# When merged rows are squared, when weight scales may be taken, and how the last tile is cut, in a streaming-encoder block

## The chip, the cores and the metric

The kernel runs on one core of one Trainium2 chip. Its time is device microseconds of one execution, and the profile is one execution of it on the same kind of core. TensorE (PE) multiplies, VectorE (DVE) and ScalarE (ACT) and GpSimd (POOL) work elementwise, SyncE (SP), ACT and POOL also issue DMAs. Each engine takes its own instructions strictly in the order in which the program gives them.

## The reference, cut to what matters

```python
x = x + 0.5 * swiglu_ffn(rms_norm(x, g1), w1_in, w1_out)          # FFN 1, 1024 rows of 1024, width 2816
h = rms_norm(x, g_mix)
o_a = sparse_attention(h) @ w_o_a                                 # three mixers read h
glu_a, glu_b = split(gelu(s5(h)) @ w_glu)
o_b = glu_a * sigmoid(glu_b)
o_m = memory_attention(h) @ w_o_m
g = sigmoid(gates(h))                                             # three gates per channel
merged = g[0] * o_a + g[1] * o_b + g[2] * o_m                     # where the branches meet
x = x + merged @ w_out
x = x + 0.5 * swiglu_ffn(rms_norm(x, g2), w2_in, w2_out)          # FFN 2
return rms_norm(x, g_final)
```

## The kernel before

Activations lie transposed: 128 channels on the partitions, 1024 positions along the free axis, handled in two halves of 512. Every product is made from two half-precision parts of each operand (high and low), as three fp16 matmuls that add up in one PSUM bank (`matmul3`). A weight block is loaded, its squares are summed on ACT and DVE, a power-of-two scale is taken from the sum, and the block is split into the two parts (ACT writes the high part, DVE the low one). The sum crosses the partitions by a tiny matmul with a matrix of ones into a bank called `ms`; this matmul stands in PE's queue like all others. An activation tile that is to be multiplied later goes the same way: `Rows.steps` squares it on ACT, takes its scale on DVE, writes the high part on ACT and the low part on DVE, a stage at each call of `Rows.more()`.

**Who sets the order.** The order of all instructions is fixed when the program is written out, by a planner with a cost model of its own (`Model`, `Sched`). Main work runs as a generator that yields after each group of matmuls; at each yield `Stream.prep` gives out steps of the next weight blocks, if the modelled time has come (`WBlock.can`) and the engine is modelled to be less than `BACKLOG` us behind. `WBlock.LATE` is an extra modelled time that must go by between a block's squares and its scale, so its `ms` matmul; it is 0 until FFN 2's Strassen part, where it becomes 2.5. If a block is wanted before its steps are done, `go` gives out all that is left at once.

**Where the branches meet** (in `mixer`, `for n in range(2 * ND)`): 16 units, for 8 slices of 128 channels and 2 halves each. A unit has 30 matmuls of 512 columns: 6 into `gb` (bank `lg`), 6 into `ga` (bank `mm`, two buffers), 6 into `pm` (bank `ao`, one buffer), 12 into `po` (bank `mm`). ACT takes each bank to SBUF: `sb` (with Tanh), `gc`, `sm`, and the output tile `m`; `sb`, `sm` and `gc` come from one ring `t2` of four buffers. DVE combines `sb` with `gc`, with its gate, `sm` with its gate, and `m` with its gate (two SBUF inputs each); POOL adds `sb` and `sm`, and then that sum to `m`. The last part (`rest`) of a unit is given out in the next unit. After the second half, `rest` calls `Rows.put` at once: ACT's square of the merged slice, which reads POOL's sum, stands in ACT's queue there, ahead of the next unit's Tanh, `gc` and `sm`. The tiles of the loop lie in `xa`, cut in 16 places of 512: gates in 0 to 8, merged slices in 9 to 14.

**Out of the mixers** (`out_stage`): 16 tiles of 512 columns, first the four tiles of two slices with the first six of eight rows, later the last two rows (`begun`, `ended`); `norm_forms` then prepares FFN 2's input (half 0 first) on DVE, ACT and POOL while PE multiplies the rest.

**FFN 2's second chunk** takes 11 rows of hidden width per tile; the first weight block is cut in 9 and 2 rows (`out_block`). Finished tiles are turned back by PE transposes, multiplied by the last gain and scaled by their norm (`final`, `turn`), and each 128 positions are stored by one DMA of 512 KB from SP. `between`, called in the midst of the next tile's matmuls, does all of a finished tile's turn; the last tile's turn comes after all matmuls.

Of the kernel before, what the change touches and what calls it, by code (L numbers as in the profile page):

```python
# [21 lines left out]
HT = 512  # L22
# [537 lines left out]
class Rows:  # L560
# [6 lines left out]
        self.inv2 = kb.const.tile([P, nk], F32, name=tag + "j")  # L567
        self.n, self.at, self.late, self.apart = 0, {}, [], False

    def put(self, k, src, mul=None):  # L570

        self.late += [self.steps(k, src, mul)]
        self.more()

    def more(self):
# [4 lines left out]
        while self.late:  # L580
            self.more()

    def steps(self, k, src, mul):
        kb, nc = self.kb, self.kb.nc
        t = kb.small.tile([P, 3], F32, name="rsc", tag="rsc", bufs=4)
        hl = self.t[k] = self.room(k)
        nc.scalar.activation(kb.junk(S), src, AF.Square, accum_out=t[:, 0:1])
        yield None
        kb.pow2(t[:, 0:1], t[:, 1:2], t[:, 2:3])
        inv = self.inv[:, k:k + 1]  # L590
        if mul is None:
            nc.vector.tensor_scalar(inv, t[:, 1:2], INV_MUL, None, op0=OP.mult)
        else:
            nc.vector.tensor_scalar(inv, t[:, 1:2], INV_MUL, mul, op0=OP.mult, op1=OP.mult)
        nc.vector.tensor_tensor(self.inv2[:, k:k + 1], inv, inv, op=OP.mult)
        if self.apart:
            yield None
        nc.scalar.activation(hl[:, 0], src, AF.Copy, scale=t[:, 2:3])
        yield None
        nc.vector.scalar_tensor_tensor(hl[:, 1], src, t[:, 2:3], hl[:, 0], op0=OP.mult, op1=OP.subtract)  # L600
        self.n, self.at[k] = k + 1, nc.t["vector"] + 0.12
# [5 lines left out]
class Builder:  # L607
# [348 lines left out]

    def out_block(self, w, rows, uses, first=0, apart=False):

        n = rows.nk - 2
        return self.rows_block(w, rows, uses, ((first, n - first), (n, 2)), apart)  # L960

    def rows_block(self, w, rows, uses, cuts, apart=False):
        return WBlock(self, [Seg([(0, w[k0 * P:(k0 + nk) * P])], nk, w.shape[1], rows, mul=0.5, k0=k0)
# [205 lines left out]
    def out_stage(self, blocks, rows, new_xo, xd_in, per, m, done, first=1, cut=(0, HT), between=None):  # L1169
# [4 lines left out]
        xo = {}  # L1174
        order = [(d, half, slice(0, HT)) for d, half in self.tail_order(ND, m)]
        d, half, _ = order.pop()
# [9 lines left out]
        def begun(n, d, half, s):  # L1186
            w = blocks[d // per]
            c = (d % per) * P
            yield from self.stream.begin(w, 1)
            acc, x, t = self.mm()[:, s], rows.x(half), xo[d, half][:, s]  # L1190
            g = w.segs[0]
            cuts = [0, *range(2, g.nk, 2), g.nk]
            for k0, k1 in zip(cuts, cuts[1:]):
                self.matmul3(acc, lambda i, k: g.hl[:, i, k, c:c + P], lambda i, k: x(i, g.k0 + k)[:, s], g.nk, ks=range(k0, k1))
                rows.more()
                if k0 == (4 if s.stop - s.start == HT else cuts[-2]) and between is not None:
                    between()
                yield None
            if len(w.segs) == 1:
                accs[n] = acc  # L1200
                return
            nc.vector.scalar_tensor_tensor(t, acc, g.inv, t, op0=OP.mult, op1=OP.add)
# [1012 lines left out]
    def mixer(self, w, xa, ss, xd_in, xd_out, after):  # L2215
# [87 lines left out]
        heads = lambda t, half: lambda i, k: t[:, 4 * half:4 * half + 4, 2 * k + i]  # L2303
        gates, mt, xf = {}, {}, xa.rearrange("p k a h t -> p (k a h t)")
        room = lambda i, n: xf[:, i * HT:(i + n) * HT].rearrange("p (j t) -> p j t", j=n)

        def g_in(n):
            if n < 2 * ND:
# [6 lines left out]
        late = []  # L2315
        for n in range(2 * ND):
            d, half = divmod(n, 2)
            b = w["go"][d // 2]
            glu, wm, wa = b.segs
            c = (d % 2) * P  # L2320
            yield from self.stream.begin(b)
            gb, ga = self.bank("lg"), self.mm()
            self.matmul3(gb, lambda i, k: glu.hl[:, i, k, 256 + c:256 + c + P], w["y"].x(half), 2)
            if late:
                late.pop()()
            yield None
            self.matmul3(ga, lambda i, k: glu.hl[:, i, k, c:c + P], w["y"].x(half), 2)
            sb, sm, gc = self.t2("sb"), self.t2("sm"), self.t2("gc")
            nc.scalar.activation(sb, gb, AF.Tanh, scale=glu.inv)
            yield None  # L2330
            w["m"].more()
# [10 lines left out]
            nc.vector.scalar_tensor_tensor(sm, tm, 1.0, sm, op0=OP.add, op1=OP.mult)  # L2342
            nc.gpsimd.tensor_tensor(sb, sb, sm, op=OP.add)
            w["m"].more()
            yield None
            self.matmul3(po, lambda i, k: wa.hl[:, i, k, c:c + P], heads(qS, half), 4, ks=range(2, 4))
            self.stream.end(b)
# [3 lines left out]
            def rest(d=d, half=half, wa=wa, po=po, ta=ta, sb=sb):  # L2351
                m = mt[d][:, half]
                nc.scalar.activation(m, po, AF.Copy, scale=wa.inv)
                nc.vector.scalar_tensor_tensor(m, ta, 1.0, m, op0=OP.add, op1=OP.mult)
                nc.gpsimd.tensor_tensor(m, m, sb, op=OP.add)
                if half == 1:
                    w["m"].put(d, mt[d].rearrange("p h t -> p (h t)"))

            late.append(rest)
            yield None  # L2360
        w["out"][0].go(("split", 0))
        late.pop()()
        self.stream.BACKLOG = 3
        nc.free.add(xa.tensor.name)
        en.close()
        xo, F = after()
        pool = m3.enter_context(tc.tile_pool(name="xo4", bufs=1, side="right"))
        xo = xo + [pool.tile([P, HT], F32, name="xo4", tag=f"xo4{i}") for i in range(3)]
        xo = iter([xo[i % len(xo)] for i in range(2 * ND)])
# [5 lines left out]
    def final(self, xt, ss, gb, out):  # L2375

        nc = self.nc
        late, sums = [], {}

        def between():  # L2380
            if late:
                turn(*late.pop(0))

        def turn(d, half, c, xn):
            n = (c.stop - c.start) // P
# [11 lines left out]
            if d == ND - 2:  # L2397
                sums[half] = self.vss[:, 4 * half:4 * half + 4]
                nc.vector.tensor_scalar(sums[half], self.row_sums(ss[half]), 1.0 / D, EPS, op0=OP.mult, op1=OP.add)
            if d == ND - 1:  # L2400
                i0 = c.start // P
                nc.vector.scalar_tensor_tensor(v, v, 1.0 / D, sums[half][:, i0:i0 + n], op0=OP.mult, op1=OP.add)
                self.rsqrt(y, v, "n")
                for i in range(n):
                    t = t0 + i
                    if i < 3 * n // 4:
                        nc.vector.tensor_scalar(xt[:, t], xt[:, t], y[:, i:i + 1], None, op0=OP.mult)
                    else:
                        nc.scalar.activation(xt[:, t], xt[:, t], AF.Copy, scale=y[:, i:i + 1])
                    nc.sync.dma_start(out[t * P:(t + 1) * P], xt[:, t])  # L2410

        def done(d, half, c, acc, w, xo):
            xn = self.t2("xn")
            nc.vector.scalar_tensor_tensor(xn[:, c], acc, w.inv, xo, op0=OP.mult, op1=OP.add)
            if d < ND - 1:
                self.square_add(ss[half], sp(xn), d == 0)
            late.append((d, half, c, xn))
            yield None

        return done, between  # L2420


@with_exitstack
def tile_hybrid_block(ctx, tc, x, mem, ffn1_norm, ffn1_w_in, ffn1_w_out, mix_norm, w_in, a_q_gain, a_k_gain, rel_bias,
# [4 lines left out]
    kb = Builder(ctx, tc)  # L2429
# [61 lines left out]
    def main():  # L2491
# [6 lines left out]
        with ExitStack() as en:  # L2498
# [19 lines left out]
            def ring(kind):  # L2518
                n[kind] += 1
                i = n[kind] - 1  # L2520
                if kind == "xo":
                    return F["xo"][i % 4]
                if kind == "gt":
                    i = 8 + 2 * (i % 2)
                    return tiles[:, i:i + 2].rearrange("p i t -> p (i t)")
                return tiles[:, i % 8]
# [12 lines left out]
            nc.gpsimd.dma_start(gb, final_norm.to_broadcast([P, D]))  # L2539
            xt = F["all"].rearrange("p n k j t -> p (n k j t)").bitcast(F32)[:, 0:S * D // P].rearrange("p (i n) -> p i n", n=D)  # L2540
            done, between = kb.final(xt, ss, gb, out[0])
            yield from kb.out_stage(b2[-1], g2, lambda: ring("xo"), xd[2], 2, 2, done, 3, between=between)
            between()

    sched.add(setup(), 1)
# [32 lines left out]
```

## Time and profile before

| | us |
|---|---|
| median of three runs (lowest, highest) | 2257.52 (2257.22, 2260.11) |
| the profiled execution's own time | 2257.12 |
| its span, first to last instruction | 2255.0 |
| PE busy in the span | 2140.5 (95%) |
| DVE, ACT, POOL busy | 1347.8, 1186.8, 396.2 |

Times in the rows are microseconds from the span's start, and mean durations are nanoseconds. A row of the timeline has start, duration, engine, line, instruction, tile written and tiles read, shapes and count; square brackets tell how long the engine stood idle before it and whose work ended that. PE's granted clock is given as a share of 2.4 GHz, so 0.5 is 1.2 GHz.

### The profile page before, as it was taken

Reading aid. Unit: us, or ns where it says so; the run is one execution under the profiler, and the core shown is the slowest. Engines: PE = TensorE matmul, PEld = TensorE weight load, DVE = VectorE, ACT = ScalarE, POOL = GpSimd, SP = SyncE. Lnnn points to the kernel's source line nnn. Section 1 sums busy time; section 2 is a strip of 40 time slices with the busy share of each in tenths; the row PEclk is TensorE's granted clock in tenths of the full one; section 3 lists DMA queues with packets and bytes.
Section 4 is the critical chain, followed back from the end, with each engine's and each line's share of the span. In section 5 each row is a group of like instructions: output and inputs, shape, how many; then the busy total and the mean of one; then the engine's idle time right before and its main releaser. Section 6 shows DMA issues by size and latency. Waiting matters only on the chain. (4 is left out here: it accounts for less than half of the span.)

```text
span 2255.0 us, 33448 instructions
## 1 busy us (share of the span) xinstructions
PE 2140.5 (95%) x12585; PEld 1141.1 (51%) x12589; DVE 1347.8 (60%) x3669; ACT 1186.8 (53%) x2367; POOL 396.2 (18%) x582
## 2 busy tenths in 40 slices
PE   6999999999999889979999999898999999999997
PEld 3555444444444556656556674333854444444443
DVE  6446852344555467677669886675756643466653
ACT  6543434344444488778877766544555432455421
POOL 1200130000000103312200004410254301344100
PEclk9999999999999999999999999999999999999999
DMA  6422231202222102123321204334111234112222
GB/s 224 120 82 82 64 103 57 63 26 80 89 89 85 52 20 79 40 66 108 122 86 58 65 37 152 117 120 119 43 57 57 70 123 125 47 57 64 81 62 93
DMA packets 204066, 185.18 MB, mean 82 GB/s; under 512 B 7376, under 2 KB 176528, under 8 KB 203264
## 3 DMA queue, kind: packets, MB, share of 16 engines
q1 hardware_dynamic: 185904, 135.84, 19.1%
q0 software_dynamic: 8416, 29.36, 4.1%
q10 hardware_dynamic: 9584, 17.85, 2.7%
q8 instruction: 98, 1.61, 0.3%
q14 instruction: 64, 0.52, 0.1%
HBM read 143.57 MB, written 40.50 MB: 82 GB/s over the span
## 5 line engine op out<-in xcount | busy, mean ns | idle before, releaser
L62 PEld LDWEIGHTS <-wh 128*128 128x128 f16 x8412 | 817.3, 98 | 949.5 <-issue 38.0
L62 PE MATMUL mm<-xa,wh 128*128 128x512 f16 x2376 | 540.0, 380 | 6.5 <-ACT xa L62 4.9
L62 PE MATMUL lg<-xa,wh 128*128 128x512 f16 x1080 | 242.6, 379 | 0.4 <-DVE xn L62 0.4
L62 ACT ACTIVATE junk<-wf 128x1024 f16<-128x1024 f32 (+3 forms) x292 | 194.0, 664 | 35.7 <-DMA wf<-in_ffn_w_in_dram 20.1
L62 PE MATMUL mm<-G,wh 128*128 128x512 f16 x960 | 210.5, 379 | 0.0
L62 DVE SCALAR_TENSOR_TENSOR wh<-wf,wsc,wh 128x1024 f16<-128x1024 f32 (+1 forms) x132 | 176.3, 1337 | 49.3 <-ACT wh L62 49.1
L62 PE MATMUL mm<-H,wh 128*128 128x512 f16 x864 | 197.3, 383 | 6.8 <-ACT wh L62 5.2
L62 PE MATMUL lg<-F,wh 128*128 128x512 f16 (+1 forms) x900 | 179.4, 353 | 0.0
L62 ACT ACTIVATE wh<-wf,wrs 128x128 f16<-128x128 f32 (+2 forms) x304 | 112.4, 438 | 103.4 <-DVE wrs L62 94.0
L62 ACT ACTIVATE wh<-wf,wsc 128x1024 f16<-128x1024 f32 (+1 forms) x132 | 139.1, 1060 | 33.3 <-DVE wsc L62 23.3
L62 PE MATMUL mm<-wh,xa 128*128 128x256 f16 (+2 forms) x1152 | 129.1, 271 | 13.9 <-ACT us L62 7.8
L62 PE MATMUL mm<-F,wh 128*128 128x512 f16 (+1 forms) x672 | 129.2, 347 | 0.0
L62 PEld LDWEIGHTS <-xa 128*128 128x128 f16 x1152 | 108.2, 106 | 32.1 <-issue 15.4
L62 DVE SCALAR_TENSOR_TENSOR wh<-wf,wrs,wh 128x128 f16<-128x128 f32 (+2 forms) x304 | 112.9, 423 | 12.7 <-ACT wh L62 11.5
L62 DVE SCALAR_TENSOR_TENSOR gt<-lg,wsc,si 128x512 f32<-128x512 f32 x44 | 33.0, 749 | 129.6 <-PE lg L62 110.5
L62 PE MATMUL ao<-F,wh 128*128 128x512 f16 x456 | 104.6, 379 | 0.0
L62 ACT ACTIVATE junk<-wk,kathr 128x1024 f16<-128x1024 f32 (+2 forms) x96 | 99.5, 1036 | 8.7 <-POOL kathr L62 6.8
L62 POOL TENSOR_TENSOR xa<-hs,xa 128x512 f16<-128x512 f32 x16 | 19.9, 1249 | 475.4 <-ACT xa L62 475.4
L62 DVE SCALAR_TENSOR_TENSOR xo<-mm,wsc,xo 128x512 f32<-128x512 f32 x44 | 33.0, 749 | 102.9 <-PE mm L62 102.9
L62 POOL TENSOR_TENSOR xa<-xa 128x512 f32<-128x512 f32 (+1 forms) x40 | 57.2, 1432 | 174.2 <-ACT xa L62 125.7
L62 ACT ACTIVATE junk<-gt 128x1024 f16<-128x1024 f32 x22 | 23.2, 1057 | 120.1 <-DVE gt L62 120.1
L62 PE MATMUL mm<-m,wh 128*128 128x512 f16 x336 | 79.9, 395 | 5.1 <-DVE wh L62 3.2
(511 smaller groups left out, 2924.8 us busy)
## 6 DMA issues: line engine op xcount, KB each, us to landing
wf<-in_ffn_w_in_dram SPq DMA_DIRECT2D x88, 512.0 KB, 4.8
xo<-xd ACTq DMA_DIRECT2D x64, 256.0 KB, 2.7
gd<-gt SPq DMA_DIRECT2D x48, 256.0 KB, 2.0
xa<-gd POOLq DMA_DIRECT2D x16, 768.0 KB, 5.0
wf<-in_ffn_w_out_dram SPq DMA_DIRECT2D x8, 1280.0 KB, 5.9
wf<-in_ffn_w_out_dram SPq DMA_DIRECT2D x7, 1408.0 KB, 5.9
wf<-in_w_in_dram SPq DMA_DIRECT2D x17, 512.0 KB, 4.8
xd<-xa SPq DMA_DIRECT2D x32, 256.0 KB, 2.4
```

The lines of the kernel that those rows point to most:

```text
L62: r = f(*a, **k)
```

## The change

Rows of the merged slices are put later: after the next unit's `sm`, and for the last slice after three more calls of `more()`. `gc` gets a place of its own in `xa`. `LATE` is 2.0 from unit 12 to the end of the loop and 3.5 from there to FFN 2's Strassen part. The last chunk's first weight block is cut in 8 and 3 rows. The last tile (slice 7, half 1) is multiplied in two parts of 256 columns; the turn of a last-slice tile becomes a generator with two stops, which the second part steps through, and `between(True)` takes one stage where `between()` takes all.

```diff
-    def put(self, k, src, mul=None):
+    def put(self, k, src, mul=None, after=0):
-        self.late += [self.steps(k, src, mul)]
+        self.late += [self.steps(k, src, mul, after)]
         self.more()
...
-    def steps(self, k, src, mul):
+    def steps(self, k, src, mul, after):
         kb, nc = self.kb, self.kb.nc
+        for _ in range(after):
+            yield None
...
-        n = rows.nk - 2
-        return self.rows_block(w, rows, uses, ((first, n - first), (n, 2)), apart)
+        n = rows.nk - (3 if apart else 2)
+        return self.rows_block(w, rows, uses, ((first, n - first), (n, rows.nk - n)), apart)
...
-                if k0 == (4 if s.stop - s.start == HT else cuts[-2]) and between is not None:
-                    between()
+                if k0 == (2 if s.start else 4) and between is not None:
+                    between(s.start > 0)
...
+        spare, ready = xf[:, 15 * HT:16 * HT], []
...
             yield from self.stream.begin(b)
+            if n == 12:
+                WBlock.LATE = 2.0
...
-            sb, sm, gc = self.t2("sb"), self.t2("sm"), self.t2("gc")
+            sb, sm, gc = self.t2("sb"), self.t2("sm"), spare
...
             nc.gpsimd.tensor_tensor(sb, sb, sm, op=OP.add)
             w["m"].more()
+            if ready:
+                w["m"].put(*ready.pop())
             yield None
...
                 if half == 1:
-                    w["m"].put(d, mt[d].rearrange("p h t -> p (h t)"))
+                    ready.append((d, mt[d].rearrange("p h t -> p (h t)")))
...
         late.pop()()
+        w["m"].put(*ready.pop(), after=3)
+        WBlock.LATE = 3.5
...
-        def between():
+        def between(step=False):
             if late:
-                turn(*late.pop(0))
+                if not step:
+                    for _ in late[0]:
+                        pass
+                if not step or next(late[0], 0) == 0:
+                    late.pop(0)
...
             if d == ND - 1:
+                yield None
                 i0 = c.start // P
                 nc.vector.scalar_tensor_tensor(v, v, 1.0 / D, sums[half][:, i0:i0 + n], op0=OP.mult, op1=OP.add)
                 self.rsqrt(y, v, "n")
+                yield None
                 for i in range(n):
                     t = t0 + i
-                    if i < 3 * n // 4:
+                    if i < (n if c.stop == HT // 2 else 3 * n // 4):
...
             xn = self.t2("xn")
+            if c.start:
+                between(True)
             nc.vector.scalar_tensor_tensor(xn[:, c], acc, w.inv, xo, op0=OP.mult, op1=OP.add)
...
-            late.append((d, half, c, xn))
+            late.append(turn(d, half, c, xn))
...
-            yield from kb.out_stage(b2[-1], g2, lambda: ring("xo"), xd[2], 2, 2, done, 3, between=between)
+            yield from kb.out_stage(b2[-1], g2, lambda: ring("xo"), xd[2], 2, 2, done, 3, cut=(0, HT // 2, HT), between=between)
+            between(True)
             between()
```

## Rows read from the trace of the kernel before

**Rows 1.** Busy time of the engines in two stretches: the loop where the branches meet, and the first tiles out of the mixers. Columns: stretch, its length, then busy time (and instructions) of PE, PE's weight loads, DVE, ACT, POOL, then the granted clock, DMA share, GB/s.

```profile
1352.00:1471.00 119.00, 106.05 (x497) 47.41 (x496) 82.08 (x144) 67.26 (x117) 57.38 (x43) 1.00 0.40 131
1471.00:1494.00 23.00, 19.35 (x83) 8.09 (x82) 16.44 (x44) 8.50 (x20) 3.93 (x3) 0.93 0.29 92
```

**Rows 2.** What PE waited for between 1345 and 1600 us: us in total, times, longest.

```profile
PE ms L62 <- ACT junk L62: 10.7, 4, 7.7
PE mm L62 <- ACT gc L62: 9.8, 6, 2.7
PE mm L62 <- DVE wh L62: 3.4, 3, 2.8
```

**Rows 3.** What ACT and DVE waited for between 1352 and 1485 us, in the same columns.

```profile
ACT junk L62 <- POOL xa L62: 37.5, 8, 6.1
DVE rsc L62 <- ACT junk L62: 17.0, 8, 2.7
```

**Rows 4.** Timeline of the loop's end: the square of a merged slice, the next `gc` and the matmul that wants its bank; then one `gc` and the DVE instruction that reads it.

```profile
1462.05 1.06 ACT L62 ACTIVATE junk<-xa 128x1024 f16<-128x1024 f32 x1 [5.44 <-POOL xa L62]
1465.11 0.67 ACT L62 ACTIVATE gc<-mm,wsc 128x512 f32<-128x512 f32 x1
1465.83 1.46 PE L62 MATMUL mm<-y,wh 128*128 128x512 f16 x6 [1.61 <-ACT gc L62]
1468.18 0.70 ACT L62 ACTIVATE gc<-mm,wsc 128x512 f32<-128x512 f32 x1
1472.50 0.68 DVE L62 SCALAR_TENSOR_TENSOR sb<-sb,gc 128x512 f32<-128x512 f32 x1
```

**Rows 5.** Timeline of the loop: DVE instructions with two SBUF inputs beside a POOL addition, and a POOL addition that DVE leaves alone.

```profile
1382.98 1.27 POOL L62 TENSOR_TENSOR xa<-xa,sb 128x512 f32<-128x512 f32 x1 [0.72 <-DVE xa L62]
1404.35 1.28 DVE L62 SCALAR_TENSOR_TENSOR m<-xa,rsc,m 128x1024 f16<-128x1024 f32 x1
1404.53 2.23 POOL L62 TENSOR_TENSOR sb<-sb,sm 128x512 f32<-128x512 f32 x1 [4.86 <-DVE sm L62]
1405.55 1.76 DVE L62 SCALAR_TENSOR_TENSOR xa<-xa 128x512 f32<-128x512 f32 x1
```

**Rows 6.** The first matmuls out of the mixers, the square of the last merged slice, and the stretch about them in the columns of the first group.

```profile
1472.64 0.82 PE L62 MATMUL mm<-m,wh 128*128 128x512 f16 x3 [0.39 <-DVE wh L62]
1476.30 7.90 PE L62 MATMUL mm<-m,wh 128*128 128x512 f16 x28 [2.84 <-DVE wh L62]
1479.47 1.06 ACT L62 ACTIVATE junk<-xa 128x1024 f16<-128x1024 f32 x1 [5.96 <-POOL xa L62]
...
1471.00:1481.00 10.00, 6.77 (x23) 2.42 (x22) 7.31 (x15) 3.66 (x9) 3.93 (x3) 0.83 0.05 5
```

**Rows 7.** Timeline ahead of FFN 2: the eviction of a mixer tile on DVE, four `ms` matmuls that waited for squares, and the stretch after the first two in the columns of the first group.

```profile
1562.20 0.74 DVE L62 SCALAR_TENSOR_TENSOR xa<-mm,wsc,xo 128x512 f32<-128x512 f32 x1
1565.73 0.16 PE L62 MATMUL ms<-wss,ones_b 128*128 128x1 bf16 x1 [7.75 <-ACT junk L62]
1566.91 0.16 PE L62 MATMUL ms<-wss,ones_b 128*128 128x1 bf16 x1 [1.02 <-ACT junk L62]
1594.68 0.16 PE L62 MATMUL ms<-wss,ones_b 128*128 128x1 bf16 x1 [0.95 <-ACT junk L62]
1595.87 0.16 PE L62 MATMUL ms<-wss,ones_b 128*128 128x1 bf16 x1 [1.02 <-ACT junk L62]
...
1566.00:1573.00 7.00, 6.08 (x16) 2.19 (x16) 2.69 (x6) 2.53 (x4) 0.00 (x0) 0.52 0.24 75
```

**Rows 8.** The fourth out block: its `ms` matmul, and the wait of its first tile.

```profile
1522.46 0.17 PE L62 MATMUL ms<-wss,ones_b 128*128 128x1 bf16 x1
1527.14 3.06 PE L62 MATMUL mm<-m,wh 128*128 128x512 f16 x12 [0.61 <-ACT wh L62]
```

**Rows 9.** The start of FFN 2's second chunk: the square of the last hidden row, and two waits of PE.

```profile
2112.02 1.06 ACT L62 ACTIVATE junk<-xa 128x1024 f16<-128x1024 f32 x1 [1.44 <-POOL xa L62]
2115.18 0.79 PE L62 MATMUL mm<-H,wh 128*128 128x512 f16 x2 [3.87 <-ACT wh L62]
2116.57 4.75 PE L62 MATMUL mm<-H,wh 128*128 128x512 f16 x16 [0.60 <-DVE wh L62]
```

**Rows 10.** The end: the last tile's first matmuls, the turn and row sums of the tile before, the last tile's eviction, multiplication by the gain and scaling, and what the DMA engines moved in 40 slices of 0.3 us from 2244 to 2256 us. Ahead of them two rows of 256-column matmuls, 24 each, one right behind the other.

```profile
1588.33 2.78 PE L62 MATMUL mm<-F,wh 128*128 128x256 f16 x24
1590.95 2.78 PE L62 MATMUL lg<-F,wh 128*128 128x256 f16 x24
...
2230.41 4.05 PE L62 MATMUL mm<-H,wh 128*128 128x512 f16 x18
2234.73 0.66 PE L62 MATMUL lg<-ident,xn 128*128 128x128 f32 x4 [0.28 <-DVE xn L62]
2236.12 1.05 PE L62 MATMUL ms<-ones,ss 128*128 128x1 f32 x8 [0.73 <-DVE ss L62]
2240.47 0.75 DVE L62 SCALAR_TENSOR_TENSOR xn<-mm,wsc,xo 128x512 f32<-128x512 f32 x1 [3.10 <-PE mm L62]
2243.69 0.69 DVE L62 TENSOR_TENSOR F<-lg,xa 128x512 f32<-128x512 f32 x1 [2.47 <-ACT junk L62]
2246.66 2.08 DVE L62 TENSOR_SCALAR F<-F,ny 128x1024 f32<-128x1024 f32 x3
...
GB/s 0 0 0 0 0 0 0 0 0 0 0 0 0 0 355 410 423 437 410 382 423 423 423 423 437 423 396 437 396 437 355 0 0 0 0 0 0 0 0 0
```

## The prediction

> **What bounds the kernel now.** I read the page's busy line first: PE is busy for 2140.5 of 2255.0 us, so what can be won at once is some 114 us of PE idle, and what PE loses at half clock. The matmuls themselves stay the same in number of columns, so every gain must come out of a wait. Next the busy time by stretch, to find where the change's places stand: in the loop where the branches meet PE is idle for 119 - 106.05 = 12.95 us, and in the next 23 us for 3.65 us [rows 1]. Then PE's waits there: 10.7 us for ACT's squares (`ms <- junk`), 9.8 us for `gc`, 3.4 us for low parts of weights on DVE [rows 2]. One level back stands what these engines waited for: ACT waited 37.5 us in eight times for POOL's sum in order to square it, and DVE 17.0 us in eight times for that square [rows 3]. The timeline joins the two: ACT stands 5.44 us in front of the square, and behind it in ACT's queue is the `gc` that starts at 1465.11 and whose end lets PE go on, 1.61 us late [rows 4]. PE's six waits for `gc` come once for each merged slice. So the loop is not bound by any engine's work but by one instruction put too early in a strictly ordered queue.
>
> **The change part by part.**
>
> *Rows put later, `gc` in its own place.* No instruction is added or taken away; the square moves behind Tanh, `gc` and `sm` of the next unit, its scale and parts one unit on. A unit has 30 matmuls at 0.216 us (256 columns take 2.62/24 = 0.109 [rows 10], 512 twice that), 6.47 us. POOL's sum comes after PE's last matmul, ACT 0.7, DVE 0.7 to 1.76 and POOL 1.27 to 2.23 us [rows 5], so 2.7 to 4.7 us into the next unit; the square now stands behind `sm`, whose matmuls end 18 x 0.216 = 3.9 us into it. So ACT's 37.5 us shrink to at most a microsecond each, and PE's 9.8 us for `gc` go. What is late next is DVE: with its waits for squares gone it has work throughout. Per two units it has eight 512-column and one 1024-column instructions with two SBUF inputs, at 1.20 us per 1024 (1404.35 to 1405.55 [rows 5]) 6.0 us, and the weight blocks' low parts, 2560 columns for four units, so 1.5 us; POOL's four additions are 4 x 1.27 = 5.1 us. Where they meet they do not overlap: POOL's 1.27 becomes 2.23 beside DVE's 1.28, and the DVE instruction behind takes 1.76, until POOL is done [rows 5]. Together 12.6 us, against PE's 12.94. That is just under, so PE's waits stay small while buffers last, but DVE ends the loop some us behind. Bounds for what remains of the 12.95: 0, and 8 (two units at 14 us, so 16 x 7.0 = 112 us less 103.5); I take 3, nearer to the lower, since PE needs only ACT's copies and is a whole unit ahead of DVE through the buffers. Gain 10.
>
> The Trainium skill ("SBUF — State Buffer", Who interferes with whom) says that a VectorE instruction with two SBUF inputs and a GpSimd instruction that reads SBUF take one port in turn, each for its whole length. The rows agree (1.76 beside 2.23), and by the rule alone the loop could not go below 8 x 12.6 = 101 us, which is under PE's 103.5; the rule speaks against a gain without remainder, which is a rival below.
>
> *Out of the mixers.* PE waits 0.39 + 2.84 us for low parts there, and its clock is granted at 0.83 over 10 us [rows 6]; a third of those 10 us at 1.2 GHz costs PE half of that time, some 1.7 to 2.1 us. The low parts are late because DVE is, at the end of a chain that ACT's square began. Now DVE comes about 4 us nearer to PE. Of 5.7 us (3.65 idle and 2.1 of clock) I take 2.7 as gained; bounds 0 and 5.7. The last square (ACT stood 5.96 us before it [rows 6]) comes three groups of matmuls later, at 3 x 1.3 = 3.9 us into the tiles; its parts are wanted by the last two rows' matmuls, 72 x 0.216 = 15.5 us in. Cover of 10 us, so nothing lost.
>
> *`LATE` 3.5.* PE stands 7.75 + 1.02 us in front of an `ms` matmul for a weight block of FFN 2 that it needs only 20 us later, and runs at a clock of 0.52 for 7 us after [rows 7], which costs some 3 us. With 3.5 us of modelled time the matmul falls behind the current tile's last 6 matmuls and one or two groups of the next. But the next tile's bank is evicted only at 1562.20 + 0.74 [rows 7], so PE stands from 1559.1 to 1563.0, and after one group at 1564.3 again until the squares are done at 1566.9. So the last tile, before done at 1566.94 + 30 matmuls at the lower clock, 1576.3, ends at 1566.9 + 18 x 0.216 = 1570.8, or some 2 us later at half clock. Gain 3.5 to 5.5; I take 4, bounds 0 (the square decides anyway) and 7 (no wait but the bank's). The later pair, 0.95 + 1.02 us [rows 7], goes for the most part: 1.5. On the other side stand the out blocks: the fourth's `ms` matmul comes 2.6 us ahead of its first tile, which still waits 0.61 us [rows 8]. With 3.5 us more it is given out only when the tile begins, and scale, high and low part of the first row stand open on the path: about 0.2 + 0.7 + 0.5 + 0.5 us less the 0.61, so 1.3, and 0.7 for the second block's last rows: 2 lost; bounds 0 and 6 (each of the three blocks 2 us).
>
> *Eight and three rows.* Nothing: PE's 3.87 and 0.60 us there end with ACT and DVE coming out of the last hidden row (its square at 2112.02, after POOL [rows 9]), with the weight's rows behind; that order stays, with one row of 0.4 us less behind it and one more in the second part, which has 15 us of cover. Bounds -0.5 and +1.
>
> *Last tile in two parts.* Until the tile's first group DVE does what it did. PE starts at 2230.41, but 18 matmuls of 256 columns end at 2232.4, and the turn of the tile before still waits for DVE, to 2234.73 [rows 10]: 2 us more of idle PE. Row sums end at 2237.0 as before; 15 matmuls end at 2238.7, the second part's 33 and two transposes at 2242.6, against 2240.3. The first part's squares and gain (half of four squares 1.6, 0.4) end at 2241.65, its inverse root 2.36 us later (2246.66 - 2243.69 - 0.61), at 2244.0; only then comes DVE's eviction of the second part (0.4 to 0.75), the first part's two scalings (1.3), the second's gain (0.4) and root (2.36) to 2248.7, and ACT's scaling to 2249.8, against 2248.7. In exchange only 1 MB is left to store, not 2: before, data moved from 2248.2 to 2253.3 at some 415 GB/s [rows 10]; now from about 2250.2 for 2.5 us, to 2252.7. Gain 0.5; bounds +2 and -4 (the 2 us bring PE to half clock, so that 48 matmuls take 5 us more).
>
> **Sum.** 10 + 2.7 + 4 + 1.5 - 2 + 0 + 0.5 = 16.7 us. Against the profiled execution's own 2257.12 us (span 2255.0 and 2.1 around it) that gives 2240.4; the runs' median is 0.4 above it, so 2241.
>
> **The rivals.**
>
> *The port takes over.* If DVE and POOL in turn need 14 us for two units in place of 12.6 (each POOL addition lengthening one DVE instruction, as in [rows 5]), the loop keeps 8 us of its waits and DVE's lag at its end stays whole: gain 5 + 0 + 4 = 9, so 2248. For it: 12.6 of 12.94 leaves little. Against: DVE stood idle for the square 17.0 us [rows 3], so it has that much to give.
>
> *All of it.* DVE keeps pace: 13 + 5.7 + 7 + 1.5 = 27, so 2230. For it: ACT's 37.5 us [rows 3] were the root of all; against: the eviction at 1562.9 [rows 7].
>
> *The squares at FFN 2's start stay in the way.* The model is 8 us off there [rows 7], more than 3.5; if DVE's normalisation sets the time anyway, `LATE` gives 0 and costs 2 to 4 on the out blocks: 2257.5 - 10 - 2.7 + 3 = 2247.
>
> *Not slower becomes slower: the single place for `gc`.* ACT can write the next `gc` only when DVE has read the last. The widest distance is 1468.18 to 1473.18, 5.0 us [rows 4], against a unit's 6.47. From 6.47 on each further microsecond holds ACT, with Tanh and `gc` behind it, in each of 16 units; at 8 us it costs 1.5 x 16 = 24 against the 16.7: 2265.
>
> *It doesn't do what it says.* The planner decides anew from shifted times; if the waits only change place (a square still ahead of POOL's sum, a block given out late), nothing is left: 2256.
>
> **How the numbers follow.** Forecast 0.42 (its own range 2235 to 2245), port 0.20, all of it 0.17, squares in the way 0.12, `gc` 0.04, no effect 0.05. The measurement of this kernel can tell 0.2%, 4.5 us, from no change, so faster means below 2253: 0.42 + 0.20 + 0.17 + 0.12 = 0.91; within 0.05; slower 0.04. The range takes in port, squares and all of it with a little on either side: 2229 to 2250; what is left out is the last two rivals and the tails, under 0.2.
>
> **What would show it.** Right: in the loop's stretch ACT's waits for POOL's sum fall from 37.5 to under 8 us and PE's for `gc` to under 2, the stretch from 119 to about 106 to 109; DVE's instructions beside POOL stay at about 1.75. Before FFN 2 PE's wait falls in two, one for an eviction by DVE. At the second chunk the 3.87 us stay. At the end PE stands about 2 us before the turn's transposes, and the last stores begin later but are done sooner. Wrong: PE's waits in the loop for `sm`, `m` or `gc` that end with DVE or POOL (the port or the single place); out blocks whose first row PE waits for by more than 2 us each; a clock of 0.5 in the last tile.

## The result and the profile after

| | before | after |
|---|---|---|
| median of the runs (us) | 2258.82 (2257.22 to 2262.76, 4 runs) | 2244.82 (2241.79 to 2246.26, 4 runs) |
| profiled execution: time, span (us) | 2257.12, 2255.0 | 2245.28, 2243.5 |
| PE's busy time (us) | 2140.5 | 2147.1 |

The ratio is 0.9932, with a 95% interval of 0.9919 to 0.9944: 14.0 us faster by the medians, where 16.7 us were forecast, and inside the range. By the profiled executions it is 11.8 us. These two hold something that the change doesn't touch: up to the loop where the branches meet PE's program is the same in both kernels, yet the loop's first matmul comes at 1352.7 us before and at 1357.1 us after (the last section returns to it). From there on the change can be read off stage by stage. Each stage goes from the first matmul of its kind to the first of the next, in the timelines of PE, read to about 0.1 us; out of the mixers the first 96 matmuls are taken by themselves:

| stage (us) | before | after | gain | forecast |
|---|---|---|---|---|
| loop where the branches meet | 118.3 | 107.7 | 10.6 | 10 |
| first 96 matmuls out of the mixers | 26.6 | 24.65 | 2.0 | 2.7 |
| rest of the mixers' output | 78.6 | 79.3 | -0.7 | 4 - 2 = 2 |
| FFN 2 to the start of its last `ao <- F` matmul | 532.4 | 526.7 | 5.7 | 1.5 |
| from there to the end | 146.3 | 148.1 | -1.8 | 0 + 0.5 |
| sum | 902.3 | 886.4 | 15.9 | 16.7 |

The page of the changed kernel, busy time of the engines:

```profile
PE 2147.1 (96%) x12622; PEld 1148.6 (51%) x12622; DVE 1352.7 (60%) x3683; ACT 1188.6 (53%) x2367; POOL 395.2 (18%) x582
```

PE is busy 6.6 us longer in a shorter span, with the same number of columns. All of it stands ahead of the loop, in work that the change doesn't touch: up to the loop's first matmul PE is busy 1290.6 us before and 1297.6 us after, from there on 849.9 and 849.4 us. The last section shows most of it to be matmuls at a lower granted clock.

**The loop.** Busy time by stretch, in the columns of [rows 1]: the loop of the changed kernel, and its last tile.

```profile
1357.00:1465.00 108.00, 104.91 (x495) 47.34 (x493) 84.84 (x159) 70.25 (x124) 55.81 (x43) 1.00 0.43 144
2219.00:2231.00 12.00, 9.46 (x57) 7.58 (x57) 4.67 (x10) 2.01 (x6) 0.00 (x0) 0.72 0.50 198
```

PE is idle for 108 - 104.91 = 3.1 us in the loop, where it was 12.95 [rows 1]. What PE waited for between 1345 and 1600 us, as in [rows 2], the five longest:

```profile
PE mm L62 <- DVE xa L62: 4.1, 1, 4.1
PE ms L62 <- DVE wj L62: 3.4, 2, 2.3
PE mm L62 <- ACT wh L62: 2.3, 2, 1.3
PE mm L62 <- ACT xa L62: 1.8, 1, 1.8
PE mm L62 <- DVE wh L62: 1.6, 1, 1.6
```

Neither `gc` (9.8 us) nor ACT's squares (10.7 us) stand there any more. `gc` now lies in `xa`, so the 1.8 us are its name here: one wait, at the loop's end. The two longest of ACT's waits between 1352 and 1485 us, as in [rows 3]:

```profile
ACT junk L62 <- POOL xa L62: 13.4, 5, 4.5
ACT m L62 <- DVE rsc L62: 10.9, 7, 2.5
```

ACT still waits for POOL's sum, 13.4 us in place of 37.5, and has a new wait for DVE's scale. These no longer hold PE, as the timeline shows:

```profile
1443.54 1.06 ACT L62 ACTIVATE junk<-xa 128x1024 f16<-128x1024 f32 x1 [3.07 <-POOL xa L62]
1444.60 0.67 ACT L62 ACTIVATE xa<-mm,wsc 128x512 f32<-128x512 f32 x1
1450.78 2.23 POOL L62 TENSOR_TENSOR sb<-sb,sm 128x512 f32<-128x512 f32 x1 [2.09 <-DVE sm L62]
1451.80 1.76 DVE L62 SCALAR_TENSOR_TENSOR xa<-xa 128x512 f32<-128x512 f32 x1
...
1463.00 1.15 ACT L62 ACTIVATE m<-xa,rsc 128x1024 f16<-128x1024 f32 x1 [2.53 <-DVE rsc L62]
1464.78 3.18 PE L62 MATMUL mm<-m,wh 128*128 128x512 f16 x14 [1.81 <-ACT xa L62]
```

The square waits 3.07 us, but at a place where the copy behind it (1444.60) holds up no matmul. Only at 1463.00 is ACT held by a row's high part with a copy for PE behind it, and that is the 1.81 us.

**The rest of the mixers' output and FFN 2's start.** Timeline of the changed kernel on PE:

```profile
1507.45 0.16 PE L62 MATMUL ms<-wss,ones_b 128*128 128x1 bf16 x1 [2.31 <-DVE wj L62]
1508.86 12.18 PE L62 MATMUL mm<-m,wh 128*128 128x512 f16 x42 [1.25 <-ACT wh L62]
...
1525.03 5.21 PE L62 MATMUL mm<-m,wh 128*128 128x512 f16 x22 [1.09 <-ACT wh L62]
...
1561.00 5.23 PE L62 MATMUL mm<-m,wh 128*128 128x512 f16 x12 [4.08 <-DVE xa L62]
...
1568.71 2.78 PE L62 MATMUL mm<-F,wh 128*128 128x256 f16 x24
...
1588.63 1.47 PE L62 MATMUL lg<-FB,wh 128*128 128x256 f16 x12
```

Ahead of FFN 2 the 7.75 + 1.02 us [rows 7] have become one wait of 4.08 us for an eviction by DVE. From the start of that wait (1561.00 - 4.08 = 1556.92) to FFN 2 it is 11.8 us with 24 matmuls, before 18.3 us with 30 (1565.73 - 7.75 = 1557.98, to 1576.27): with 0.216 us for a matmul 6.6 us lost in place of 11.8, a gain of 5.2. On the other side stand the out blocks, with waits of 2.31, 1.25 and 1.09 us where there were 0.17, 0.61 and 0.61, and 42 matmuls that took 12.18 us, not 42 x 0.216 = 9.1: a loss of 5.9 in all up to that wait. Together that is the -0.7 of the table.

**The last tile**, in the timeline of PE, beside [rows 10]:

```profile
2216.96 2.13 PE L62 MATMUL mm<-H,wh 128*128 128x256 f16 x18
2221.30 1.05 PE L62 MATMUL lg<-ident,xn 128*128 128x128 f32 x4 [2.20 <-DVE xn L62]
2222.68 1.86 PE L62 MATMUL ms<-ones,ss 128*128 128x1 f32 x8 [0.33 <-DVE ss L62]
2224.41 2.08 PE L62 MATMUL mm<-H,wh 128*128 128x256 f16 x9
```

PE stands 2.20 us ahead of the turn's transposes, and behind that the row sums take 1.86 us, where they took 1.05; nine matmuls of 256 columns take 2.08 us, at 0.109 each they would take 1.0. Over these 12 us the granted clock is 0.72 (the stretch above). From the tile's first matmul to the span's end it is 26.5 us (2216.96 to 2243.5), before 24.6.

### The profile page after: what moved, and what is told of

It reads as the page before. It is cut to its first block, busy times and chain, and to the rows that moved or that the text cites. A ratio compares the mean times of both kernels' runs of the same rounds, so it can differ in the third digit from the quotient of the medians.

```text
span 2243.5 us, 33554 instructions
## 1 busy us (share of the span) xinstructions
PE 2147.1 (96%) x12622; PEld 1148.6 (51%) x12622; DVE 1352.7 (60%) x3683; ACT 1188.6 (53%) x2367; POOL 395.2 (18%) x582
## 5 line engine op out<-in xcount | busy, mean ns | idle before, releaser
L62 DVE SCALAR_TENSOR_TENSOR wh<-wf,wsc,wh 128x1024 f16<-128x1024 f32 (+1 forms) x132 | 177.3, 1345 | 49.8 <-ACT wh L62 49.7
L62 PE MATMUL mm<-H,wh 128*128 128x512 f16 (+1 forms) x879 | 194.9, 376 | 6.6 <-ACT wh L62 5.2
L62 POOL TENSOR_TENSOR xa<-hs,xa 128x512 f16<-128x512 f32 x16 | 19.9, 1247 | 476.8 <-ACT xa L62 476.8
L62 PE MATMUL mm<-m,wh 128*128 128x512 f16 x336 | 80.4, 398 | 10.7 <-DVE xa L62 4.1
L62 ACT ACTIVATE xa<-mm,wsc 128x512 f32<-128x512 f32 x51 | 34.8, 682 | 104.8 <-PE ms L62 60.9
```

The source lines that it names most:

```text
L62: r = f(*a, **k)
```

## The experiments

My theory after the result: the square in front of ACT's queue was the loop's whole loss, and `gc`'s place a small part of it; `LATE` is good ahead of FFN 2 and a loss on the out blocks; the cut of the last tile is a gain in itself, turned into a loss by the half clock that a new wait of PE brings; eight and three rows do nothing. The rivals: `gc`'s place made the loop; DVE, no longer held up, would do without `LATE`; the cut tile costs by its work, not by the wait. All kernels start from the changed one. `LATE` of 2.0 from unit 12 and the three calls by which the last slice's rows come later stand in all of them, so what these two give alone is not shown. The stages (before and after again as the scale); each ratio is to runs of the kernel before that were taken beside that row, with medians of 2261.0 to 2261.6 us for the experiments and 2258.82 for the changed kernel, so that medians of different rows may differ by 2 to 3 us for that alone:

| us | loop | out of the mixers | FFN 2 | end | median of runs | ratio to before, 95% |
|---|---|---|---|---|---|---|
| before | 118.3 | 105.3 | 532.4 | 146.3 | 2258.82 | |
| after | 107.7 | 103.9 | 526.7 | 148.1 | 2244.82 | 0.9932 (0.9919 to 0.9944) |
| `gc` in the ring | 110.1 | 101.8 | 526.7 | 148.0 | 2248.53 | 0.9953 (0.9935 to 0.9971) |
| rows put at once | 122.7 | 104.1 | 528.4 | 149.0 | 2261.66 | 1.0006 (0.9996 to 1.0016) |
| last tile whole | 107.7 | 101.9 | 526.6 | 148.4 | 2244.85 | 0.9930 (0.9912 to 0.9948) |
| `LATE` for FFN 2's first four blocks alone | 107.6 | 98.1 | 532.7 | 148.6 | 2245.95 | 0.9939 (0.9921 to 0.9956) |
| `LATE` for all of FFN 2 | 107.7 | 97.6 | 526.7 | 148.8 | 2242.04 | 0.9912 (0.9898 to 0.9927) |
| and the turn behind the eviction | 107.6 | 98.3 | 528.3 | 143.6 | 2233.00 | 0.9875 (0.9861 to 0.9890) |
| the same, last tile whole | 107.7 | 98.0 | 528.5 | 146.7 | 2238.10 | 0.9896 (0.9880 to 0.9913) |
| nine and two rows | 107.7 | 101.9 | 526.6 | 150.3 | 2246.13 (one run) | |
| no `LATE` behind the loop | 107.6 | 102.9 | 532.1 | 148.8 | 2249.91 | 0.9952 (0.9935 to 0.9969) |

**`gc` back in the ring.**

```diff
-            sb, sm, gc = self.t2("sb"), self.t2("sm"), spare
+            sb, sm, gc = self.t2("sb"), self.t2("sm"), self.t2("gc")
```

> The changed kernel, with gc taken from the ring t2 again (its output is the same). Loop = from the first matmul of gb to the first matmul out of the mixers; 118.3 us before the change, 107.7 after it. If the late square alone made the loop shorter, the loop stays within 1.5 us of 107.7. If the place for gc made it (ACT's waits for POOL's sums were 8.7 us at sm), the loop goes back by 5 us or more, to 113 or longer. If the single place holds ACT up, the loop gets shorter than 106.

Measured: the loop takes 110.1 us, 2.4 more, and of PE's waits between 1345 and 1640 us one is back:

```profile
PE mm L62 <- ACT gc L62: 4.1, 4, 1.8
```

Behind these stand ACT's waits for POOL at `sm`, 5.1 us in five, where the changed kernel has none. The 110.1 us lie between the two forecasts: of the loop's 10.6 us the place of `gc` is 2.4. It is the smaller part, but not nothing: its four waits follow from the buffer alone, with the rows still put late.

**Rows put at once.**

```diff
-                if half == 1:
+                if half == 1 and d < ND - 1:
+                    w["m"].put(d, mt[d].rearrange("p h t -> p (h t)"))
+                elif half == 1:
                     ready.append((d, mt[d].rearrange("p h t -> p (h t)")))
```

The last slice is still put late.

> The changed kernel, with the rows of a merged slice put at once again, as before (the last slice alone stays late); gc keeps its own place. If the square's place in ACT's queue is the cause of the loop's waits, ACT again stands over 25 us in front of the squares, PE waits for gc about 8 us, and the loop goes back to 116 to 119 us. If the ring was the cause, the loop stays at 108 to 111.

Measured: the loop takes 122.7 us, and the gain of the whole change is gone (ratio 1.0006). ACT's waits between 1352 and 1485 us are nearly those of the kernel before again (37.5 us):

```profile
ACT junk L62 <- POOL xa L62: 32.7, 7, 6.0
```

and the matmuls that want a bank wait for the copy behind the square, in the timeline of PE:

```profile
1426.12 1.58 PE L62 MATMUL mm<-y,wh 128*128 128x512 f16 x6 [4.10 <-ACT xa L62]
...
1427.57 2.72 PE L62 MATMUL ao<-qmS,wh 128*128 128x512 f16 x6
```

PE's waits for it are 11.4 us in six. That the square ahead of POOL's sum was the loop's loss is shown: with it back, the other parts of the change win nothing in the loop. The first 96 matmuls out of the mixers take 27.0 us, about as before (26.6; 24.65 in the changed kernel). The loop is even longer than before (118.3) and than forecast (116 to 119). Of these 4.4 us PE's busy time is 3.0 (108.4 against 105.4), and the granted clock shows it: behind the 4.10 us six matmuls take 2.72 us where six take 1.46 us as a rule. The other 1.4 are more idle time.

**Last tile whole.**

```diff
-            yield from kb.out_stage(b2[-1], g2, lambda: ring("xo"), xd[2], 2, 2, done, 3, cut=(0, HT // 2, HT), between=between)
+            yield from kb.out_stage(b2[-1], g2, lambda: ring("xo"), xd[2], 2, 2, done, 3, between=between)
```

> The changed kernel, with the last tile multiplied whole. End = from the last tile's first matmul to the end of the span; 24.6 us before the change, 26.5 after it. If the cut brings PE's 2.2 us of idle and the half clock behind it, the end goes back to 24.6 and PE's clock stays full in it, so 2 us less in all. If the end was only longer by chance of the clock, it stays at 26 or more.

Measured: by the medians no difference from the changed kernel (2244.85 against 2244.82), with runs that overlap (2240.6 to 2245.2). The timeline of PE tells more:

```profile
2213.50 4.05 PE L62 MATMUL mm<-H,wh 128*128 128x512 f16 x18
2217.83 0.66 PE L62 MATMUL lg<-ident,xn 128*128 128x128 f32 x4 [0.28 <-DVE xn L62]
2219.22 1.05 PE L62 MATMUL ms<-ones,ss 128*128 128x1 f32 x8 [0.73 <-DVE ss L62]
```

The 18 matmuls of 512 columns last until DVE is nearly there, so PE waits 0.28 us, and the row sums take 1.05 us at full clock. From the tile's first matmul to the end it is 25.3 us, against 26.5 with the cut and 24.6 in the kernel before. From that matmul to the last scaling it is 16.3 us in both whole-tile kernels, so the 0.7 us between these two kernels stand in the storing (9.0 and 8.3 us), and what makes them is not shown. As it stands the cut loses 1 to 2 us in the tail, which the medians can't tell from nothing; the 2 us in all that were expected are not seen in them.

**`LATE` for FFN 2's first four blocks alone, and for all of FFN 2.** The first sets `LATE` to 0 behind the loop and to 3.5 on FFN 2's first four blocks; the second sets it to 3.5 again from FFN 2's start up to the Strassen part:

```diff
-        WBlock.LATE = 3.5
+        WBlock.LATE = 0.0
...
+        for p in a[:PLAIN + 1]:
+            p.LATE = 3.5
...
+        WBlock.LATE = 3.5
         gts = [early(f) for f in range(PLAIN)]
```

(The last two lines stand in the second only.)

> The changed kernel, with LATE at 0 again for the blocks out of the mixers and 3.5 for FFN 2's first four blocks alone. Out = from the first matmul out of the mixers to FFN 2's first; 105.3 us before the change, 103.9 after it. If LATE costs the out blocks their lead (2.31 + 1.25 + 1.09 us of PE waits and some 3 us at half clock) and FFN 2's blocks give the gain, the third and fourth out block's waits fall under 1.5 us together, the wait for the eviction of 4 us stays, and out takes 97 to 100 us. If the two are not separable (the waits come from DVE being late), out stays at 103 to 105.

> The changed kernel with LATE 0 for the blocks out of the mixers, and 3.5 for FFN 2's first four blocks and from FFN 2's start until the Strassen part (in the run before, the fifth block had 0 again). If that run lost its 6 us in FFN 2 by the fifth block's two waits for squares (3.9 us) and the half clock behind them (2.1 us), FFN 2 (its first matmul to the last one of S4) goes from 532.7 to 527 us with out at 98, and the whole is some 5 us faster than the changed kernel. If LATE for the out blocks also served FFN 2 in another way, FFN 2 stays over 530.

Measured: with no `LATE` on the out blocks the output of the mixers takes 98.1 and 97.6 us, against 103.9 in the changed kernel and 101.8 to 101.9 in three others that have it. So the out blocks pay 4 to 6 us for `LATE`; the waits are alike in these four profiles, and the 2 us between them are the clock behind these waits and behind the one for the eviction. The first of the two, in the timeline of PE:

```profile
1505.40 6.04 PE L62 MATMUL mm<-m,wh 128*128 128x512 f16 x18 [1.91 <-ACT wh L62]
...
1554.75 4.19 PE L62 MATMUL mm<-m,wh 128*128 128x512 f16 x12 [4.08 <-DVE xa L62]
...
1623.57 0.16 PE L62 MATMUL ms<-wss,ones_b 128*128 128x1 bf16 x1 [2.55 <-ACT junk L62]
1625.08 0.16 PE L62 MATMUL ms<-wss,ones_b 128*128 128x1 bf16 x1 [1.34 <-ACT junk L62]
```

Of the out blocks' three waits one of 1.91 us is left (under 1.5 was expected). The 4.08 us for the eviction are the same. But the fifth block of FFN 2, which now has no `LATE`, makes PE wait 2.55 + 1.34 us for squares, and FFN 2 goes from 526.7 to 532.7 us; with `LATE` there too it is 526.7 again.

**No `LATE` behind the loop.** One line, 3.5 to 0.0, in place of both.

> The changed kernel with LATE at 0 for every block behind the loop: the out blocks and FFN 2's alike. Theory (LATE takes away PE's stand before FFN 2 and for its later pair, and has its price in the out blocks): the out blocks come as in the run with LATE for FFN 2 alone, but PE stands 6 to 8 us for ACT's square before an ms matmul ahead of FFN 2, in place of 4.08 us for the eviction, with half clock behind it; the out stage then takes 100 to 104 us (98.1 with LATE for FFN 2 alone, 103.9 in the changed kernel), FFN 2 530 to 533 us (526.7 with LATE throughout), and the median is 2248 to 2254 us. Rival (DVE, which the loop no longer holds up, has the square done in time without LATE, so that LATE is only a cost): no such wait over 2 us, out stage 95 to 99 us, FFN 2 527 to 529, median 2239 to 2243 us.

Measured: both of the old stalls are back where they were, in the timeline of PE:

```profile
1556.50 0.16 PE L62 MATMUL ms<-wss,ones_b 128*128 128x1 bf16 x1 [7.75 <-ACT junk L62]
1557.68 0.16 PE L62 MATMUL ms<-wss,ones_b 128*128 128x1 bf16 x1 [1.02 <-ACT junk L62]
...
1584.97 0.16 PE L62 MATMUL ms<-wss,ones_b 128*128 128x1 bf16 x1 [0.95 <-ACT junk L62]
1586.15 0.16 PE L62 MATMUL ms<-wss,ones_b 128*128 128x1 bf16 x1 [1.02 <-ACT junk L62]
```

These are the four numbers of [rows 7] to the hundredth, though the loop ends 10.7 us sooner after its start; the rival, by which ACT would be in time without `LATE`, falls. The mixers' output takes 102.9 us, 4.6 to 5.3 more than with `LATE` for FFN 2 (97.6 to 98.3 in four runs), and FFN 2 532.1, 5.4 more, of which some 1.3 are the clock behind a wait that all kernels have (last section). By the medians `LATE` behind the loop is worth 5.1 us as the change has it (2249.91 to 2244.82), and 7.9 without the out blocks (to 2242.04); by the ratios it is 4.5 and 9.0, with intervals that overlap in the first case and not in the second.

**The turn behind the eviction.** On top of `LATE` for all of FFN 2: in `final` the inverse root and the scalings of slice 7, half 0 come behind the eviction of slice 6, half 1, and half of its scalings go to ACT. Its core:

```diff
         def between(step=False):
             if late:
+                step = step or whose[0] == (ND - 1, 0)
...
+            while late and whose[0] == (ND - 1, 0):
+                between(True)
             late.append(turn(d, half, c, xn))
+            whose.append((d, half))
...
-                    if i < (n if c.stop == HT // 2 else 3 * n // 4):
+                    if i < (n if c.stop == HT // 2 else n // 2):
```

and the same with the last tile whole.

> The run before this, and at the end the first half's last turn in stages: its inverse root and its scalings come behind the eviction and square sum of tile (6, 1), two of its four scalings on ACT. The last tile stays in two parts. End = last tile's first matmul to the end of the span; 24.6 us before the change, 26.5 after it. If the 2.2 us of PE idle and the half clock behind it are what the cut lost, PE waits under 0.5 us before that turn, its clock stays full, and the end takes 20 to 22 us. If storing sets the end, it stays at 24 or more.

> As the run before this, with the last tile whole. If the cut itself is worth something once its stall is gone (half the stores earlier, a shorter chain), the end takes 23 to 24.5 us here against 20 to 22 there. If the cut is worth nothing, both take the same.

Measured: 2233.00 us (2231.0 to 2235.4) with the cut, 2238.10 (2237.5 to 2239.3) without. Timeline with the cut:

```profile
2210.69 2.13 PE L62 MATMUL mm<-H,wh 128*128 128x256 f16 x18
2210.89 0.75 DVE L62 SCALAR_TENSOR_TENSOR xn<-mm,wsc,xo 128x512 f32<-128x512 f32 x1 [0.95 <-PE mm L62]
2212.66 0.60 PE L62 MATMUL lg<-ident,xn 128*128 128x128 f32 x4
2213.09 1.04 PE L62 MATMUL ms<-ones,ss 128*128 128x1 f32 x8
```

The eviction stands at 2210.89, right behind its tile, and the transposes need not wait; the row sums take 1.04 us, so the clock is full again. From the tile's first matmul to the end it is now 21.6 us, with the tile whole 23.2. Without the new order it was 26.5 and 25.3. So the cut is worth 1.6 us in the tail as soon as it brings no wait of PE, and its loss came from the wait and the clock behind it, not from its work. The medians give 5.1 us between the two, but only these 1.6 can be put down to the cut. Of the profiles' difference 3.1 us stand in the ends (143.6 against 146.7): the other 1.5 arise at the second chunk's start, where both wait 3.87 us and the whole-tile kernel then has a wait of 0.78 in place of 0.35 us and 1.1 us more of lower clock. Another 2.1 stand ahead of the loop, which begins at 1356.6 in place of 1354.5 us. This kernel is the fastest of all, 1.25% below the one before. Against `LATE` for all of FFN 2 alone the new order is worth 5.2 us by the ends (148.8 to 143.6); the medians give 9.0, and where the rest comes from the profiles don't show.

**Nine and two rows.**

```diff
-        n = rows.nk - (3 if apart else 2)
+        n = rows.nk - 2
```

> The changed kernel with the last chunk's first block in nine and two rows again. At the chunk's start PE waits 0.75, 3.87 and 0.6 us before the change and 0.75, 3.87 and 0.44 after it. If the cut does nothing, the three waits stay within 0.3 us of these. If it served the start, the middle wait grows by 0.5 us or more.

Measured: 2246.13 us in a single run, so without an interval. PE's waits at the last chunk's start, in the timeline:

```profile
2100.57 1.03 PE L62 MATMUL mm<-H,wh 128*128 128x512 f16 x2 [3.87 <-ACT wh L62]
2101.96 6.14 PE L62 MATMUL mm<-H,wh 128*128 128x512 f16 x16 [0.35 <-DVE wh L62]
```

In the changed kernel they are 3.87 and 0.44 us, before 3.87 and 0.60 [rows 9]. The waits are the same, so the cut of the weight does nothing that can be seen. That 16 matmuls take 6.14 us is the granted clock behind the 3.87 us: the kernel before has the same cut, and they took 4.75 there [rows 9]. This 1.4 us is most of what its end (150.3) is longer.

## Why the prediction was right, and where not

**The loop: right in place, cause and size.** It forecast 10 us and 3 us of idle PE left; 10.6 and 3.1 were measured, and putting the rows at once takes it all back. One of its signs was too strict: ACT's waits for POOL's sum stayed at 13.4 us, not under 8. PE's wait for `gc`, 1.8 us at the loop's end, is under the 2 that it named. PE's waits for `gc` before were six, so for six of the eight slices and not for each, which changes nothing. DVE is indeed late next (ACT's 10.9 us for `rsc`), and is so off the path until the last unit. The rival of the port falls: DVE still takes 1.76 us beside POOL's 2.23, which agrees with the Trainium skill ("SBUF — State Buffer", Who interferes with whom), but the loop ended 3.1 us above PE's work, not 8. That of `gc`'s single place falls too; the place is a gain of 2.4. Of the others, the one by which all is won falls by the 3.1 us left in the loop and the 4.08 ahead of FFN 2, and the one of the squares by the run without `LATE`.

**Out of the mixers: right**, 2.0 of 2.7, and gone with the rows put at once. Waits of 1.55, 0.75 and 0.89 us are left there; the 1.81 us ahead of the first matmul count with the loop.

**`LATE`: right in mechanism, both sides too small.** The wait that takes the place of the old one is the one named, DVE's eviction, and as long as worked out (forecast 1559.1 to 1563.0, 3.9 us; measured 4.08). The second wait that it expected behind that one, for the squares, didn't come. The gain ahead of FFN 2 is 5.2, forecast 4. The term that was mis-sized is the out blocks' 2 us: 5.9 in this profile, at the upper bound. The step named the second and the fourth block and took no loss on the third; the third's scale came 2.31 us late and its first row 1.25 later still. And it priced waits alone: some 3 us of the 5.9 are the 42 matmuls behind these waits at half clock. In three other profiles with the same waits the stretch to the third of them is 1.3 us shorter, so that much of the 5.9 is this execution's. The later pair was put at 1.5, the sum of its waits; from FFN 2's first matmul to the one behind that pair it was 23.9 us (1576.27 to 1600.17), and is 19.9 (1568.71 to 1588.63), so 4.0 less. Again what is missing is the clock, as the kernel before shows in its timeline of PE:

```profile
1595.89 2.03 PE L62 MATMUL mm<-FB,wh 128*128 128x256 f16 x12
1597.71 2.62 PE L62 MATMUL mm<-F,wh 128*128 128x256 f16 x12
```

These 24 matmuls take 4.28 us, to 1600.17, in place of 2.62. The price stood in the rows: the prediction took a clock of 0.52 into account behind the first pair and not behind the second.

**Eight and three rows: right**, nothing.

**The last tile: wrong by the bound that it named.** "Gain 0.5; bounds +2 and -4 (the 2 us bring PE to half clock, so that 48 matmuls take 5 us more)": the 2 us came (2.20), and half clock with them, so the tail is 1.9 us longer. The step that failed is the choice of full clock for the row sums and the 48 matmuls behind the wait, and the clock that it gave as a sign of being wrong was seen. It fell for a part of them only: the row sums and the next 15 matmuls take 4.88 us, where they take 2.55 in the kernel with the turn moved, so 2.3 us more. From the twentieth of the 48 on they come 0.109 us apart again, so the 5 us of the bound did not come. The forecast had the last scaling on ACT 18.3 us behind the tile's first matmul (2230.41 to 2248.7); it begins 20.7 us behind it, in the timeline of ACT:

```profile
2237.62 1.15 ACT L62 ACTIVATE F<-F,ny 128x1024 f32<-128x1024 f32 x1 [2.73 <-DVE ny L62]
```

The later part, with one half of the store left to do, went as worked out: 5.9 us from there to the end, before 8.3 (from 2246.66).

**The sum** of 16.7 against 15.9 is closer than its terms: the out blocks, the first tiles and the last tile were 3.9 + 0.7 + 2.3 = 6.9 us worse, the loop and the two pairs 0.6 + 1.2 + 4.2 = 6.0 better, and 1.5 of that is not the change's, as the last section shows. That the sum came so near is luck in part. (The sum of the rival of the squares gives 2247.8, not 2247; its chance doesn't hang on that.)

## What to carry to other kernels

In a queue in strict order, an instruction that waits for a slow partner costs what stands behind it, so move it behind whatever the bound engine needs next, even at the price of more waits of its own. A wait of PE is to be priced with the clock behind it: in this kernel some waits of 2 us cost as much again. And a switch that is right for one group of blocks (those of FFN 2, with 20 us of cover) can be a loss for the next (the out blocks, with 2.6), so set it for each group.

## What was not expected of the hardware

**The clock behind one and the same wait.** Some 230 us into FFN 2 all kernels have the same instructions on PE and wait alike, for 0.87, 1.31 and 0.28 us in a row. The 22 matmuls behind these waits, in the timeline of PE of the changed kernel, first, and of the one with the turn moved, second:

```profile
1800.13 4.92 PE L62 MATMUL mm<-H,wh 128*128 128x512 f16 x22 [0.28 <-DVE wh L62]
```

```profile
1791.77 6.61 PE L62 MATMUL mm<-H,wh 128*128 128x512 f16 x22 [0.28 <-DVE wh L62]
```

4.92 us in six of the eleven profiles, and 6.45 to 6.61 in four others, among them the kernel before (in the eleventh, without the 0.28 us, 24 matmuls are one row, 7.15). So 1.5 us of FFN 2's 5.7 (6.45 against 4.92) were these executions' clock, not the change. Behind the 2.20 us in the last tile it was no chance: the seven profiles with that wait all have row sums of 1.69 to 1.87 us, the four without it 0.95 to 1.05. Length alone doesn't decide either: PE stood 2.7 us for `gc` in the kernel before [rows 2], and the granted clock of that loop was 1.00 [rows 1].

**The stretch ahead of the loop.** The loop's first matmul comes between 1352.7 and 1358.7 us in the eleven profiles. One stretch well ahead of it, in the columns of [rows 1], of the kernel before and then of the changed one:

```profile
1000.00:1050.00 50.00, 44.96 (x457) 35.17 (x453) 33.04 (x111) 38.39 (x85) 4.51 (x19) 1.00 0.18 56
```

```profile
1000.00:1050.00 50.00, 45.75 (x472) 37.08 (x469) 28.95 (x97) 34.69 (x78) 2.60 (x12) 0.94 0.11 33
```

The granted clock is 1.00 in the one and 0.94 in the other, in work that is the same on PE. Of the 4.4 us by which the changed kernel's loop begins later, 3.0 arise about the start of this stretch, behind the same two waits in both kernels (2.93 us, then 2.63 and 2.64): the 12 matmuls of 256 columns behind each take 1.47 us before, 2.32 and 2.71 us after. Another 1.0 lies in the first 80 us of the program. What decides the clock behind such a wait no run here shows. The 6 us between the profiles are as much as most terms of this change, and so a single profile is read by stages that begin with the change, not by its span.
